# Attention over two sets of key tiles, near keys and keys of the same residue modulo four, joined by an exchange of maxima and sums

## The chip, the cores and the metric

The kernel runs on one core of a Trainium2 chip. The core has five engines that work side by side, each through its own instructions in order: TensorE (PE, matmuls and transposes; its weight loads are listed as PEld), VectorE (DVE), ScalarE (ACT), GpSimd (POOL) and SyncE (SP), which here only issues DMA transfers. PE writes into PSUM, of which the kernel's pools take eight banks of 128 partitions by 512 fp32 numbers; everything else lies in SBUF, and tensors too large for it go to DRAM and back by DMA. The metric is the device time of one execution in microseconds, as the median of several runs.

## What is computed

A block of one layer on a sequence of 1024 tokens with 1024 channels: a gated convolution branch and an attention branch, both gated and added to the input, and then a feed-forward part with a short convolution. Only the attention matters here. Each of 16 heads of 64 channels attends over three groups of keys:

```python
DILATION_GROUPS = ((128, 1), (512, 4), (2048, 16))
...
def dilated_window_attention(q, k, v, slopes, window, dilation):
    n_back = window // dilation
    ...
    scores = jnp.einsum('nbqhd,nbkhd->nbhqk', qb, kc)
    steps = (jnp.arange(ATTN_BLOCK)[:, None] + ATTN_BLOCK) - jnp.arange(2 * ATTN_BLOCK)[None, :]
    valid = (steps >= 0) & (steps <= n_back)
    ...
    dist = (steps * dilation).astype(jnp.float32)
    scores = scores - slopes[:, None, None] * dist
    scores = jnp.where(valid[None, :, None], scores, -jnp.inf)
    m = jnp.max(scores, axis=-1, keepdims=True)
    p = jnp.exp(scores - m)
    den = jnp.sum(p, axis=-1)
    o = jnp.einsum('nbhqk,nbkhd->nbqhd', p, vc) / jnp.swapaxes(den, 2, 3)[..., None]
    lse = jnp.swapaxes(m[..., 0] + jnp.log(den), 2, 3)
    return from_sub(o), from_sub(lse)
...
        mix = jax.nn.softmax(jnp.stack(lses), axis=0)
        o = jnp.einsum('gbsh,gbshd->bshd', mix, jnp.stack(outs))
```

The first group takes every key up to 128 tokens back, the second the keys of the same residue modulo 4 up to 512 back, the third those of the same residue modulo 16 as far back as there are any. Mixing the groups by the softmax of their log-sums is the same as one softmax in which a key counts once for each group that it is in; so a key's score gets the logarithm of its count added, and keys in no group are left out.

## The kernel before

All matrix products are made in fp32 halves: a factor is split into a high part of the type fp32r and the rest, the low part, and the products that matter are added up. A "split" is a copy by ACT (L86) and a subtraction by DVE (L87).

**Ahead of the attention** the projections to q, k and v are computed in tiles of 128 tokens (L150). `qkv_tail` turns each q and k tile by four PE transposes (L679) and stores high and low halves in DRAM (`dq`, `dk`); `qkv_head` stores v, high half and low half side by side, in `dv`. A first part of the gate products also lies there.

**The attention** takes the heads one after the other in eight slots each, 128 slots for 16 heads. Slot i of a head is the block of 128 queries i, and its work is:

- `score`: PE multiplies the queries with all keys of the blocks 0 to i, two matmuls (high, L776, and low half, L777, of the keys) per 512 columns; DVE (L781) adds the mask row, which holds slope, distance and logarithm of the count, and takes the row's extreme. A head has 1 + 2 + ... + 8 = 36 tiles of 128 x 128.
- `powers`: ACT takes the exponential and its row sum (L786).
- `share`, one slot later: DVE inverts the sum (L789), POOL scales the rows (L790).
- `flip`, BACK = 5 slots later: PE transposes the scaled tiles (L796) into one bank per key block and half of the queries, and ACT and DVE split the result into `ph` and `pl`.
- `weigh`, one slot after the flip: PE multiplies `ph` and `pl` with the values (L810, L811), the values' high and low halves being the 128 columns of the loaded weights; the output's upper and lower 64 rows are added in `result` (L821, L822) and stored in DRAM (`do`).

Between these PE works on **filling steps**: `side_steps` yields the remaining gate products and the output product of the convolution branch, three matmuls of 512 columns a step (L122 to L124). The table FILL says how many steps a slot takes (13.64 over the eight slots of a head), SHARE which part of them comes ahead of the flips. The halves of their weights are made beside it, one piece of 512 columns a slot: the high half by ACT (L194), the low half by POOL (L187).

The order on PE, DVE and ACT is written out by hand in the slot loop; SP's and POOL's is set by a scheduler. `head(h)` issues the seven loads of a head (queries, keys high and low for two halves of the partitions, mask), two slots into the head before it; they need the buffers of the head before that. `values(h)` loads the values. PSUM holds two double banks for scores (`psA`) and four banks (`psB`) for flips, outputs and filling steps.

**Behind the attention** `merge` multiplies the attention output with its weights and then, by DVE, with the gates (L913).

Of the kernel before, what the change touches and what calls it, by code (L numbers as in the profile page):

```python
# [21 lines left out]
P = 128  # L22
D = 1024
T = 1024
# [10 lines left out]
FILL = (1.17, 2.65, 1.40, 1.48, 1.25, 2.34, 1.64, 1.71)  # L35
# [24 lines left out]
def block_kernel(ctx: ExitStack, tc: tile.TileContext, x, xT, w_first, g1, g2, pack, mask,  # L60
# [100 lines left out]
    dv = [dr.tile([P, 8, 8, P], F32R, name=f"dv{i}") for i in range(2)]  # L161
# [20 lines left out]
    low_by = [dve]  # L182

# [6 lines left out]
    def piece_high(age=0):  # L190

        if pieces and count[2] - pieces[0][3] >= age:
            hi, lo, src, _ = pieces.popleft()
            act.activation(hi, src, AF.Copy)  # L194
            half_done.append((hi, lo, src))
# [394 lines left out]
    with tc.tile_pool(name="ph1", bufs=1, reuse_waits="tile") as p1, ExitStack() as rest:  # L590
# [65 lines left out]
        def qkv_head(ch, tt, ps):  # L656
            kind, g8 = ch % 3, ch // 3
            psv = ps.rearrange("p (h d) -> p h d", h=8)
            if kind == 2:
                vt = t4(f"v_{ch}_{tt}", F32R).rearrange("p (h s d) -> p h s d", h=8, s=2)  # L660
                split(vt[:, :, 0, :], vt[:, :, 1, :], psv)
                spill(dv[g8][:, :, tt, :], vt.rearrange("p h s d -> p h (s d)"))
# [12 lines left out]
        def qkv_tail(ch, tt, qn):  # L675
            kind, g8 = ch % 3, ch // 3
            pt = turn_ps(f"qt_{ch}_{tt}")
            for j in range(4):
                pe.transpose(pt[:, j * P : (j + 1) * P], qn[:, j * P : (j + 1) * P], ident)  # L679
# [34 lines left out]
        def head(h):  # L714
# [5 lines left out]
            m = pl.tile([P, T], F32, tag="m", name=f"m_{h}")  # L720
# [41 lines left out]
    psA = ctx.enter_context(tc.tile_pool(name="psA2", bufs=2, space=PSUM, reuse_waits="tile"))  # L762

    with tc.tile_pool(name="ph2", bufs=1, reuse_waits="tile") as p2:
        vals = {}

        def values(h):
            vals[h] = p2.tile([P, 8, P], F32R, tag="v", bufs=2, name=f"v_{h}")
            fetch(vals[h], dv[h // 8][:, h % 8, :, :])

        def score(h, tiles, i):
            q, kh, kl, m = tiles
            nk = (i + 1) * P
            s = big_ps(f"s_{h}_{i}")[:, P if i == 4 else 0 :]
            for c0, n in ((0, 384), (384, 256)) if i == 4 else [(c, min(512, nk - c)) for c in range(0, nk, 512)]:
                pe.matmul(s[:, c0 : c0 + n], q[:, i * P : (i + 1) * P], kh[:, c0 : c0 + n], start=True, stop=False)  # L776
                pe.matmul(s[:, c0 : c0 + n], q[:, i * P : (i + 1) * P], kl[:, c0 : c0 + n], start=False, stop=True)  # L777
            pt = p2.tile([P, nk], F32, tag=f"p{i}", bufs=1, name=f"p_{h}_{i}")
            st = p2.tile([P, 32], F32, tag="st", bufs=4, name=f"st_{h}_{i}")
            u0 = 896 - i * P  # L780
            dve.tensor_tensor_reduce(out=pt, in0=s[:, :nk], in1=m[:, u0 : u0 + nk], scale=-1.0, scalar=3e38,  # L781
                                     op0=ALU.add, op1=ALU.min, accum_out=st[:, 0:1])
            return pt, st

        def powers(pt, st):
# [681 lines left out]
```

## Time and profile before

| what | us |
| --- | --- |
| median of three runs | 1731.57 (1731.49 to 1732.05) |
| the profiled execution | 1732.16 |
| its span, first to last instruction | 1730.3 |
| first score to last exponential of the attention | 521.2 to 876.7 |
| ACT's last output copy of the attention | 898.4 |

The profile comes from one execution. Its page lists the busy time of each engine, the chain of work that ended last, and the costliest groups of instructions; the trace behind it can be asked for groups by line and shape, for waits, and for all instructions in order of time. A row of a timeline gives the start and the duration in us, the engine, the line, the operation, what it writes and reads, and shapes. An "idle before" behind an instruction is time in which its engine had nothing to do, with what released it; on an engine that isn't the bottleneck it costs nothing.

### The profile page before, as it was taken

What the parts mean: (1) busy time and instruction counts of PE and PEld (TensorE: products, weight loads), DVE (VectorE), ACT (ScalarE), POOL (GpSimd) and SP (SyncE); (2) the same over time, 40 slices, a digit from 0 to 9 for tenths busy, and PEclk for the clock granted to TensorE, in tenths of its full rate; (3) what the DMA queues carried; (4) which work ended last, traced back from release to release, by engine and by line L of the source; (5) the groups of instructions that cost most, each with busy time, mean ns of one, the idle gap of its engine ahead of it and who ended that gap; (6) DMA issues with size and microseconds to landing.
All of it is one profiled execution on the core that took longest, in us unless ns stands there. A gap on an engine that the chain in (4) does not pass through costs nothing.

```text
span 1730.3 us, 22656 instructions
## 1 busy us (share of the span) xinstructions
PE 1719.1 (99%) x8112; PEld 1432.8 (83%) x8112; DVE 1276.6 (74%) x1722; ACT 858.3 (50%) x1318; POOL 466.6 (27%) x351
## 2 busy tenths in 40 slices
PE   9999999999999999999999999999999999999999
PEld 7888888888888888888888888888888888888887
DVE  5999999989845666666645564887767777789863
ACT  5533345554336666776654332554445445533431
POOL 0068739999412333563410000000000000000000
PEclk9999999999999999999999999999999999999999
DMA  8232264463468656776546585622222222499851
GB/s 321 112 107 96 87 227 150 140 189 91 129 231 249 173 163 177 200 233 177 159 142 220 174 323 187 225 98 92 80 84 80 92 85 74 146 342 319 294 176 49
DMA packets 150417, 289.57 MB, mean 167 GB/s; under 512 B 12320, under 2 KB 61728, under 8 KB 150048
## 3 DMA queue, kind: packets, MB, share of 16 engines
q1 hardware_dynamic: 148576, 284.97, 50.5%
q10 hardware_dynamic: 1728, 3.15, 0.5%
q8 instruction: 64, 1.05, 0.3%
q14 instruction: 49, 0.40, 0.1%
HBM read 208.38 MB, written 79.69 MB: 166 GB/s over the span
## 4 chain that ended last, share of the span: by engine, by line
PE 96%; DMA 3%; DVE 0%; ACT 0%; issue 0%; SPq 0%; ACTq 0%
PE qkv L150 14%; PE dx L1299 7%; PE xz L130 6%; PE xz L132 6%; PE xz L131 6%; PE dy L1299 5%; PE wo L150 5%; PE pp L796 3%; PE glugv L349 3%; PE gate L122 2%; PE y L132 2%; PE y L131 2%; PE y L130 2%; PE gate L123 2%; PE gate L124 2%; PE uxz L130 2%
## 5 line engine op out<-in xcount | busy, mean ns | idle before, releaser
L630 DVE SCALAR_TENSOR_TENSOR work<-apad,pk,work 128x1024 f32<-128x1024 f32 x188 | 241.5, 1285 | 3.6
L87 DVE TENSOR_TENSOR pl<-pp,ph 128x512 fp32r<-128x512 f32 x192 | 101.1, 554 | 80.6 <-ACT ph L86 80.6
L790 POOL TENSOR_SCALAR p<-p,st 128x128 f32<-128x128 f32 (+7 forms) x128 | 96.2, 752 | 191.7 <-DVE st L789 172.3
L781 DVE CUSTOM_DVE_ANT_0 p<-s,m 128x128 f32<-128x128 f32 (+7 forms) x128 | 96.8, 756 | 55.6 <-PE s L777 42.8
L86 ACT ACTIVATE ph<-pp 128x512 fp32r<-128x512 f32 x192 | 87.3, 489 | 100.6 <-PE pp L796 99.4
L150 PE MATMUL qkv<-hi_qkv,hT 128*128 128x512 f32 x384 | 115.1, 393 | 0.0
L1202 DVE SCALAR_TENSOR_TENSOR u<-u,pk 128x1023 f32<-128x1023 f32 x88 | 112.3, 1278 | 1.0 <-ACT u L1200 0.7
L621 POOL TENSOR_TENSOR part<-prod,part 128x1024 f32<-128x1024 f32 x43 | 103.7, 2413 | 19.4 <-ACT prod L620 16.6
L786 ACT ACTIVATE p<-p,st 128x128 f32<-128x128 f32 (+7 forms) x128 | 99.2, 775 | 5.3 <-DVE st L781 2.8
L796 PE MATMUL pp<-ident,p 128*128 128x128 f32 x576 | 84.4, 273 | 0.1
L150 PEld LDWEIGHTS qkv<-hi_qkv,hT 128*128 128x128 f32 x384 | 71.4, 188 | 14.5
L796 PEld LDWEIGHTS pp<-ident,p 128*128 128x128 f32 x576 | 69.9, 140 | 15.7 <-ACT ya L248 0.3
L87 DVE TENSOR_TENSOR lo_uv<-raw_uv,hi_uv 128x1024 fp32r<-128x1024 f32 x20 | 24.5, 1226 | 78.9 <-ACT hi_uv L86 78.9
L150 PE MATMUL wo<-hi_wo,mT 128*128 128x512 f32 x256 | 80.1, 391 | 0.0
L810 PE MATMUL o<-ph,v 128*128 128x512 f32 x192 | 74.6, 392 | 0.1
L130 PE MATMUL xz<-blk_t,hi_s3g 128*128 128x512 f32 x176 | 68.6, 390 | 0.7 <-ACT xc L1176 0.7
L130 PE MATMUL xz<-h2left,hi_uv 128*128 128x512 f32 x176 | 68.7, 390 | 0.0
L132 PE MATMUL xz<-h2left,lo_uv 128*128 128x512 f32 x176 | 68.5, 389 | 0.0
L131 PE MATMUL xz<-blk_t,hi_s3g 128*128 128x512 f32 x176 | 68.5, 389 | 0.0
L132 PE MATMUL xz<-blk_t,lo_s3g 128*128 128x512 f32 x176 | 68.5, 389 | 0.0
L131 PE MATMUL xz<-h2left,hi_uv 128*128 128x512 f32 x176 | 68.5, 389 | 0.0
L150 PE MATMUL qkv<-lo_qkv,hT 128*128 128x512 f32 x192 | 68.4, 392 | 0.0
(387 smaller groups left out, 5110.0 us busy)
## 6 DMA issues: line engine op xcount, KB each, us to landing
wr<-w_down SPq DMA_DIRECT2D x45, 512.0 KB, 5.8
gr<-dff SPq DMA_DIRECT2D x62, 256.0 KB, 5.0
raw_qkv<-w_qkv SPq DMA_DIRECT2D x24, 512.0 KB, 3.9
dff<-u SPq DMA_DIRECT2D x22, 512.0 KB, 2.6
raw_uv<-w_up SPq DMA_DIRECT2D x21, 512.0 KB, 3.3
raw_ug<-w_up SPq DMA_DIRECT2D x20, 512.0 KB, 3.2
m<-mask SPq DMA_DIRECT2D x16, 512.0 KB, 7.5
q<-dq SPq DMA_DIRECT2D x32, 256.0 KB, 5.5
```

What stands on the lines that cost most here:

```text
L87: by.tensor_tensor(out=lo, in0=src, in1=hi.bitcast(F32), op=ALU.subtract)
L130: pe.matmul(o, wh[:, k, :], bh[:, k, :], start=(start and k == 0), stop=False, skip_group_check=not start)
L131: pe.matmul(o, wh[:, k, :], bl[:, k, :], start=False, stop=False, skip_group_check=not start)
L132: end = pe.matmul(o, wl[:, k, :], bh[:, k, :], start=False, stop=(k == 3), skip_group_check=not start)
L150: pe.matmul(ps, l, r[:, k % 2, :], start=(n == 1), stop=(n == 3 * KT))
L621: pool.tensor_tensor(out=a[:, CW - 1 :] if j == CW - 1 else part, in0=prods[j % 3], in1=part, op=ALU.add)
L630: dve.scalar_tensor_tensor(out=a[:, CW - 1 :] if j == CW - 1 else work, in0=a[:, j : j + T], scalar=w(c, j), in1=part if j == n else work, ...
L781: dve.tensor_tensor_reduce(out=pt, in0=s[:, :nk], in1=m[:, u0 : u0 + nk], scale=-1.0, scalar=3e38, op0=ALU.add, op1=ALU.min, accum_out=st[ ...
L786: act.activation(pt, pt, AF.Exp, bias=st[:, 0:1], scale=-1.0, accum_out=st[:, 1:2])
L796: pe.transpose(pp[:, qb * P : (qb + 1) * P], pts[qb][:, kt * P : (kt + 1) * P], ident)
L1202: dve.scalar_tensor_tensor(out=acc[:, d:], in0=src[:, : T - d], scalar=w(2 - d), in1=acc[:, d:], op0=ALU.mult, op1=ALU.add)
L1299: pe.matmul(banks[n], a[:, c], b[:, d], start=(start and i == 0 and m == 0), stop=(stop and i == nf - 1 and m == 2), skip_group_check=True)
```

## The change

The keys of a query are now taken as two sets, and each has its own row maximum and row sum.

**Near keys:** the block of the query and the one before it, n - 1 and n, so 15 tiles a head. **Keys of the same residue modulo four:** the 512 queries of one half (b = 0 or 1) and one residue r make a block of 128, with the 128 (b = 0) or 256 (b = 1) keys of that residue up to there, 4 x (1 + 2) = 12 tiles. Together 27. The mask has 512 columns, 256 per set. The first group of the reference is counted in the first set, the other two in the second.

To have the keys of one residue together, `qkv_tail` writes its transposes into PSUM so that inside a block of 128 tokens residue comes ahead of place. The queries of one residue out of four blocks are gathered on POOL (`order`), two copies a head. A slot n = 4b + r then scores near block n and residue block (b, r), both in one bank, with four matmuls and two passes of DVE and of ACT.

The rows of the two sets stand in different order over the partitions. So the maxima and sums (16 numbers per partition and set) go through DRAM: `exchange` makes two stores and two loads, and each set receives the other's numbers. MERGE = 3 slots into the next head DVE takes the common extreme (`factor_first`), ACT its exponential, and DVE the factors (`factor_last`). POOL scales the rows with them from slot 8 + BACK - 1 after the head's first on, flips begin at slot 8 + BACK, and there is one flip and one bank a slot, of 4, 3 or 2 tiles. The transposes of residue tiles write into PSUM with a step of 32, so that their columns stand in the order of the outputs. The low half `pl` meets only the high half of the values, 64 columns.

The values are fetched twice a head, in both orders. High halves of the filling steps' weights are now made by DVE in this stage. Scores and outputs share four PSUM banks (`psH`). The filling steps are spread by a table of three rates: 2.8 a slot up to slot 12, 1.53 up to the end of the scores, then 2.0.

```diff
-FILL = (1.17, 2.65, 1.40, 1.48, 1.25, 2.34, 1.64, 1.71)
+FILL = (2.8, 1.53, 2.0)
+MERGE = 3
...
             for j in range(4):
-                pe.transpose(pt[:, j * P : (j + 1) * P], qn[:, j * P : (j + 1) * P], ident)
+                pe.transpose(pt[:, j * P : (j + 1) * P].rearrange("p (r j) -> p j r", r=4), qn[:, j * P : (j + 1) * P],
+                             ident)
...
+        def order(h, b):
+            classes[h % 2, b] = t = p2.tile([P, 512], F32R, tag=f"q{b}", bufs=2 - b, name=f"q{b}_{h}")
+            q = tiles[h][0][:, 512 * b : 512 * b + 512]
+            pool.tensor_copy(t.rearrange("d (r j a) -> d r j a", a=4, r=4), q.rearrange("d (a r j) -> d r j a", a=4, r=4))
+
+        def score(h, n):
...
+            for i, k in enumerate((kh, kl)):
+                pe.matmul(s[:, c], q[:, n * P : (n + 1) * P], k[:, ks], start=(i == 0), stop=(i == 1))
+            by_class = lambda t: t.rearrange("d (i r j) -> d r i j", i=8, r=4)[:, r]
+            e = slice(256 if b else 384, 512)
+            for i, k in enumerate((kh, kl)):
+                pe.matmul(s[:, e], classes[h % 2, b][:, r * P : (r + 1) * P], by_class(k)[:, : 4 * b + 4],
+                          start=(i == 0), stop=(i == 1))
...
+        def exchange(h):
+            st = stats[h]
+            far = lambda i: dstat[i][h].rearrange("(r j) (a f) -> (j a) r f", r=4, a=4)
+            own = lambda i: st[:, i, 8:16, :].rearrange("p (r b) s -> p r (b s)", r=4)
+            sp.dma_start(dstat[0][h], st[:, 0, 0:8, :])
+            sp.dma_start(far(1), own(0))
+            sp.dma_start(own(1), far(0))
+            sp.dma_start(st[:, 1, 0:8, :], dstat[1][h])
+
+        def factor_first(h):
...
+            dve.tensor_tensor(out=w[:, 2], in0=st[:, 0, :, 0], in1=st[:, 1, :, 0], op=ALU.min)
+            dve.tensor_tensor(out=w[:, 0:2], in0=w[:, 2:3].to_broadcast([P, 2, 16]), in1=st[:, :, :, 0], op=ALU.subtract)
+            act.activation(w[:, 0:2], w[:, 0:2], AF.Exp)
...
+        def factor_last(h, w):
...
+            dve.tensor_tensor(out=st[:, :, :, 1], in0=w[:, 0:2], in1=st[:, :, :, 1], op=ALU.mult)
+            dve.tensor_tensor(out=w[:, 2], in0=st[:, 0, :, 1], in1=st[:, 1, :, 1], op=ALU.add)
+            dve.reciprocal(w[:, 2], w[:, 2])
+            dve.tensor_tensor(out=w[:, 0], in0=w[:, 0], in1=w[:, 2], op=ALU.mult)
...
+            for j, t in enumerate(srcs):
+                o = pp[:, j * P : (j + 1) * P]
+                pe.transpose(o.rearrange("p (a j) -> p j a", a=4) if j < 2 - x else o, t, ident)
...
+            for i, t in enumerate(parts):
+                m = DH if i else P
+                pe.matmul(view(o[:m]), v[:, :m], t, start=(start and i == 0), stop=(stop and i == 0),
+                          skip_group_check=True)
...
+                if n == 0 and 0 < h <= H:
+                    exchange(h - 1)
+                if n == 5 and h < H:
+                    values(h)
+                s0 = at - 7 - BACK
+                if s0 >= 0 and s0 % 8 < 7 and s0 // 8 < H:
+                    for i, k in SHARES[s0 % 8]:
+                        share(s0 // 8, i, k)
+                first = n == MERGE and 0 < h <= H
+                if first:
+                    w_now = factor_first(h - 1)
                 fill(rate * SHARE)
                 flips = []
...
+                s1 = at - 8 - BACK
+                if 0 <= s1 < 8 * H:
+                    flips.append(flip(s1 // 8, s1 % 8))
                 for w in pend:
                     done = weigh(*w) or done
                 pend = flips
-                late = None
+                if first:
+                    factor_last(h - 1, w_now)
```

The order of PE in the middle of the stage, before. One flip bank `pp` is filled by four transposes of the probabilities `p`, and the weighing adds into `o` from `ph` and `pl` (buffer numbers: head, half, key block):

```order
L796 MATMUL pp_5_0_0_5714<-ident_70,p_5_0_5520 128x128
L796 MATMUL pp_5_0_0_5714<-ident_70,p_5_1_5540 128x128
L796 MATMUL pp_5_0_0_5714<-ident_70,p_5_2_5596 128x128
L796 MATMUL pp_5_0_0_5714<-ident_70,p_5_3_5636 128x128
L810 MATMUL o_4_1_5619<-ph_4_1_6_5682,v_4_5183 128x256
L811 MATMUL o_4_1_5619<-pl_4_1_6_5683,v_4_5183 128x256
L810 MATMUL o_4_1_5619<-ph_4_1_7_5688,v_4_5183 128x128
L811 MATMUL o_4_1_5619<-pl_4_1_7_5689,v_4_5183 128x128
```

The same place in the changed kernel, with `p1` the residue tiles, `p0` the near ones, and `v1`, `v0` the values in their orders:

```order
L865 MATMUL pp_4_2_5937<-ident_70,p1_4_2_5430 128x32x4
L865 MATMUL pp_4_2_5937<-ident_70,p1_4_6_5577 128x32x4
L865 MATMUL pp_4_2_5937<-ident_70,p0_4_2_5428 128x128
L865 MATMUL pp_4_2_5937<-ident_70,p0_4_3_5458 128x128
L880 MATMUL o_4_0_5904<-ph_4_1_5900,v1_4_5539 128x4x32
L880 MATMUL o_4_0_5904<-pl_4_1_5901,v1_4_5539 64x4x32
L880 MATMUL o_4_1_5907<-ph_4_1_5900,v1_4_5539 128x4x32
L880 MATMUL o_4_1_5907<-pl_4_1_5901,v1_4_5539 64x4x32
L880 MATMUL o_4_0_5904<-ph_4_1_5900,v0_4_5538 128x256
L880 MATMUL o_4_0_5904<-pl_4_1_5901,v0_4_5538 64x256
```

Two of the four transposes now have an output in 32 steps of 4, one flip feeds both halves of the outputs, and every second matmul of the weighing has 64 output rows.

The queue of SP where the loads of a head stand, before (head 10):

```order
L156 DMA kh_10_6701<-dk1_0_80 64x1024
L156 DMA q_10_6700<-dq1_0_76 64x1024
L156 DMA kl_10_6702<-dk1_1_81 64x1024
L156 DMA q_10_6700<-dq1_1_77 64x1024
L156 DMA kh_10_6701<-dk1_0_80 64x1024
L156 DMA kl_10_6702<-dk1_1_81 64x1024
L725 DMA m_10_6703<-mask 128x1024
```

And in the changed kernel (loads of head 6, exchange of head 4, whose numbers are `st_4`, through `dst0` and `dst1` in DRAM):

```order
L157 DMA q_6_5721<-dq0_0_74 64x1024
L157 DMA kh_6_5722<-dk0_0_78 64x1024
L157 DMA kl_6_5723<-dk0_1_79 64x1024
L157 DMA q_6_5721<-dq0_1_75 64x1024
L828 DMA dst0_4_88<-st_4_5337 128x16
L829 DMA dst1_4_104<-st_4_5337 128x4x4
L157 DMA kh_6_5722<-dk0_0_78 64x1024
L157 DMA kl_6_5723<-dk0_1_79 64x1024
L830 DMA st_4_5337<-dst0_4_88 128x4x4
L831 DMA st_4_5337<-dst1_4_104 128x16
L732 DMA m_6_5724<-mask 128x512
```

The stores and the loads of the exchange now stand inside this burst, and the mask stands behind them.

DVE in the fourth slot of head 5, the changed kernel: the passes over the scores of slot 3 (`s_5_3`), the merging of head 4 (`w_4`), and between its two parts the split of a flipped tile of head 3:

```order
L815 ISA p0_5_3_5772,st_5_5642<-s_5_3_5767,m_5_5415 128x256
L815 ISA st_5_5642 128x1
L815 ISA p1_5_3_5774,st_5_5642<-s_5_3_5767,m_5_5415 128x128
L815 ISA st_5_5642 128x1
L836 TENSOR_TENSOR w_4_5776<-st_4_5337 128x16
L837 TENSOR_TENSOR w_4_5776<-w_4_5776,st_4_5337 128x32
L88 TENSOR_TENSOR pl_3_6_5788<-pp_3_6_5783,ph_3_6_5787 128x384
L843 TENSOR_TENSOR st_4_5337<-w_4_5776,st_4_5337 128x32
L844 TENSOR_TENSOR w_4_5776<-st_4_5337 128x16
L845 RECIPROCAL w_4_5776<-w_4_5776 128x16
L846 TENSOR_TENSOR w_4_5776<-w_4_5776 128x16
```

Before, a slot had one such pass, one reciprocal and its splits there, and nothing that waits for a transfer of the same head.

186 lines of the change are left out of this document (114 added, 72 removed).

## The prediction

> **What bounds the kernel now.** I read the page's head and its chain first, then the busy time by stage, then the waits of TensorE alone.
>
> ```profile
> span 1730.3 us, 22656 instructions
> ...
> PE 1719.1 (99%) x8112; PEld 1432.8 (83%) x8112; DVE 1276.6 (74%) x1722; ACT 858.3 (50%) x1318; POOL 466.6 (27%) x351
> ...
> PE 96%; DMA 3%; DVE 0%; ACT 0%; issue 0%; SPq 0%; ACTq 0%
> ```
>
> TensorE (PE) is busy for 99% of the span and makes up 96% of the chain that ended last. Next come the stage of the change (by windows: us, then PE, PEld, DVE, ACT, POOL, each busy us and count, granted clock, DMA share, GB/s) and the only wait of PE in it.
>
> ```profile
> 540.00:870.00 330.00, 328.92 (x1856) 281.70 (x1855) 209.99 (x565) 227.04 (x514) 143.05 (x162) 1.00 0.65 181
> ```
>
> ```profile
> PE s L777 <- DMA kl<-dk: 0.9, 1, 0.9
> ```
>
> In 330 us of attention PE rests for 1 us, at full clock, while VectorE (DVE) is 64% busy, ScalarE (ACT) 69%, GpSimd (POOL) 43%. So the price of the change is what it does to PE's own time, plus any new wait that reaches PE. Busy microseconds don't price a matmul, because matmuls overlap; the distance between starts does. The timeline, PE and its weight loads (PEld), start and duration in us:
>
> ```profile
> 704.47 0.49 PE L810 MATMUL o<-ph,v 128*128 128x512 f32 x1
> ...
> 704.80 0.40 PE L811 MATMUL o<-pl,v 128*128 128x512 f32 x1
> ...
> 705.04 0.40 PE L810 MATMUL o<-ph,v 128*128 128x512 f32 x1
> ...
> 709.04 0.33 PE L776 MATMUL s<-kh,q 128*128 128x384 f32 x1
> ...
> 709.21 0.34 PE L777 MATMUL s<-kl,q 128*128 128x384 f32 x1
> ...
> 709.38 0.29 PE L776 MATMUL s<-kh,q 128*128 128x256 f32 x1
> ...
> 709.51 0.28 PE L777 MATMUL s<-kl,q 128*128 128x256 f32 x1
> ...
> 709.63 0.40 PE L122 MATMUL gate<-b_again,hi_gt 128*128 128x512 f32 x1
> ...
> 709.87 0.40 PE L123 MATMUL gate<-b_again,hi_gt 128*128 128x512 f32 x1
> ...
> 720.33 0.22 PE L776 MATMUL s<-kh,q 128*128 128x128 f32 x1
> 720.34 0.19 PEld L777 LDWEIGHTS s<-kl,q 128*128 128x128 f32 x1
> 720.39 0.27 PE L777 MATMUL s<-kl,q 128*128 128x128 f32 x1
> 720.44 0.19 PEld L122 LDWEIGHTS gate<-b_again,hi_gt 128*128 128x128 f32 x1
> 720.50 0.45 PE L122 MATMUL gate<-b_again,hi_gt 128*128 128x512 f32 x1
> 720.55 0.19 PEld L123 LDWEIGHTS gate<-b_again,hi_gt 128*128 128x128 f32 x1
> ...
> 742.67 0.22 PE L776 MATMUL s<-kh,q 128*128 128x128 f32 x1
> ```
>
> From start to start: 512 columns 0.23 us, 384 0.17, 256 0.12. A matmul of 128 columns streams in 0.06 (720.33 to 720.39), but the loads behind it stand 0.10 and 0.11 apart (720.34, 720.44, 720.55), so in a row of short ones each costs the load, 0.105. The first matmul after transposes costs 0.33 instead of 0.23 (704.47 to 704.80). The last row is the first score of the next head: one head takes 742.67 - 720.33 = 22.34 us. The table FILL puts 13.64 filling steps of three 512-column matmuls beside it, 13.64 x 3 x 0.23 = 9.4 us, which leaves **12.9 us a head of attention proper**. The forms by line and one row of the chain count it:
>
> ```profile
> L776 PE MATMUL s<-kh,q x192: 218/337/442, 521.2 to 873.6; 128*128 128x512 f32 x80, 128*128 128x256 f32 x48, 128*128 128x384 f32 x48, 128*128 128x128 f32 x16
> ```
>
> ```profile
> L810 PE MATMUL o<-ph,v x192: 222/397/497, 538.3 to 897.5; 128*128 128x512 f32 x96, 128*128 128x384 f32 x32, 128*128 128x256 f32 x32, 128*128 128x128 f32 x32
> ```
>
> ```profile
> 546.03 0.87 PE pp L796 x8
> ```
>
> L777 and L811 repeat these forms with the low half. A head has 22 matmuls of 512, 10 of 384, 10 of 256 and 6 of 128: 22 x 0.23 + 10 x 0.17 + 10 x 0.12 + 6 x 0.085 (short ones stand in pairs here, 720.33 to 720.50) = 8.5 us. The 36 transposes take 36 x 0.87 / 8 = 3.9 us. Together 12.4; the missing 0.5 is the change from transposes to matmuls, eight times a head, which stays.
>
> **The change on PE.** Scores: 10 matmuls of 128 and 22 of 256, 10 x 0.105 + 22 x 0.12 = 3.7 us. The weighing: 12 of 256, 1.44 us, and 15 pairs of 128 columns, whose low half now loads only 64 columns of the values (the 64-row outputs of L880 in the changed order). A full load costs 0.105. A load of 64 columns stands nowhere in this trace: its matmul costs at least its streaming, 0.06, and at most a full load, 0.105. I take 0.06, because half of the measured load, 0.053, is below the streaming. The pairs then cost 15 x 0.165 = 2.5 us (at the upper end 3.15). Transposes: 27 x 0.109 = 2.9. So 3.7 + 1.44 + 2.5 + 2.9 + 0.5 = 11.05 us against 12.9: 1.85 a head, **29.5 us over 16 heads** (at the upper end 1.2 and 19). Notable is how little of it is columns: a quarter of the score and weigh columns goes, but the matmuls grow from 48 to 74 and become load-bound, and over half of the gain is the nine transposes, 16 us. The filling steps are the same matmuls, only spread otherwise (2.8 a slot until the first weights exist, 1.53, then 2.0): nothing.
>
> The strided outputs: 12 of the 27 transposes of a head, 192 in all, and the 128 of L679 write PSUM with a step of 32 elements.
>
> ```profile
> L679 PE MATMUL qt<-ident,qn x128: 270/272/330, 261.7 to 491.2; 128*128 128x128 f32 x128
> ```
>
> No matmul of before writes so. I bound the extra between nothing and one transpose more, 0.109, and take nothing: a transpose costs twice the 0.06 in which 128 columns stream, so its output has time to spare. [...] The strided reads and writes of keys, values and outputs keep runs of 32 elements; I cost them at nothing, with the gain or loss of a matmul hidden in the range.
>
> **The change on the other engines.** They stay beside PE as long as each has less than PE's head, 12.24 x 0.69 + 11.05 = 19.5 us. Groups by form, count, busy us and mean ns:
>
> ```profile
> L786 ACT ACTIVATION_READ_ACCUMULATOR p<-p,st 128x1 f32 x128 | 24.7, 193 | 0.0
> ...
> L786 ACT ACTIVATE p<-p,st 128x256 f32<-128x256 f32 x16 | 8.1, 504 | 0.4 <-DVE st L781 0.2
> ...
> L786 ACT ACTIVATE p<-p,st 128x128 f32<-128x128 f32 x16 | 6.3, 394 | 0.2 <-DVE st L781 0.2
> ...
> L781 DVE CUSTOM_DVE_ANT_0 p<-s,m 128x256 f32<-128x256 f32 x16 | 6.8, 422 | 6.9 <-PE s L777 6.7 <-issue 0.3
> ...
> L781 DVE CUSTOM_DVE_ANT_0 p<-s,m 128x128 f32<-128x128 f32 x16 | 4.6, 289 | 6.6 <-DMA m<-mask 2.6 <-PE s L777 2.3 <-PE pp L796 1.7
> ```
>
> ```profile
> L194 ACT ACTIVATE hi_co<-raw_co 128x512 fp32r<-128x512 f32 x16 | 10.0, 622 | 0.0
> ...
> L86 ACT ACTIVATE ph<-pp 128x512 fp32r<-128x512 f32 x96 | 53.9, 597 | 59.2 <-PE pp L796 58.0 <-ACT ya L248 0.4 <-PE o L811 0.4
> ```
>
> ACT: 16 exponentials where there were 8: 11 x 0.504 + 5 x 0.394 + 16 x 0.193 = 10.6 us a head; the splits fall by a quarter, to some 4.3 (a 512-column one is 0.597); the 0.62 us high halves of the weights go to DVE. With outputs and gates about 17 us a head of durations, as before, and durations overlap (now they fill 69% of 22.34, 15.4 us). So ACT's share rises to about 79% of 19.5. DVE: 11 x 0.422 + 5 x 0.289 and the reads, six small factor instructions, some 2.75 casts and a quarter fewer splits: about as much as now, 14.2 us, plus at most 2, so 73 to 83%. POOL has 57% rest today and gains two reorderings of the queries. None becomes the bound, but the slack of a slot (2.44 us) shrinks; I allow PE 0.3 us a head for it, 5 us.
>
> **The new wait.** DVE's minimum at L836 (L836, L838 and L880 are lines of the changed kernel) needs four transfers, two after two, and behind it on DVE stand the split of the flipped tile and the factors; behind the exponential of L838 on ACT stand the split's high half and two exponentials. PE needs that split one slot later; POOL's scaling waits for the factors, with about 3.6 us for 1.7 us of work. On SP's queue the four stand among the seven loads of the next-but-one head, whose last three or so wait behind them. Rows of that burst, and the time from issue to landing:
>
> ```profile
> 719.04 0.45 SPq L156 DMA_DIRECT2D kh<-dk  x1
> ...
> 722.78 0.53 SPq L725 DMA_DIRECT2D m<-mask  x1
> ```
>
> ```profile
> kl<-dk SPq DMA_DIRECT2D x32, 256.0 KB, 6.7
> ...
> dq<-qh SPq DMA_DIRECT2D x16, 256.0 KB, 2.6
> ```
>
> After a head's last score DVE and ACT need about 3 us. Two hops follow, each between 2.6 us (quiet) and 6.7 (in the burst): arrival 8.2 to 16.4 us after that score. DVE asks at 3 slots plus 1 us into the next head, 10.5 us after it, and PE feels it some 2.5 us later. So the hops may take 10 us. I take 9, since the burst's first half is ahead of one hop and its second half ahead of the other: no wait. Each us beyond costs 16 us. [...]
>
> **Sum.** The profiled execution took 1732.16 us, 1.9 around its span. 1732.2 - 29.5 + 5 = 1707.7; the median of before lies 0.6 below that execution, so **1707 us**.
>
> **Rivals.** *The exchange is late.* [...] One us late costs 16: 1723. Chance 0.13, half of it no longer faster. *Strided PSUM writes slow the transposes* (the other side): 320 transposes; at 0.109 more, 34.9 us, 1742, slower than before; it cancels the gain from 24.5 / 320 = 0.077 us each. [...] Chance 0.16. *The gain is smaller than its columns say:* the 64-column loads are no cheaper, or ACT's and DVE's waits take another 10 us: 1717 to 1720. For it: nothing in the trace is started faster than every 0.10 in a row. Chance 0.21. *The forecast*, 1699 to 1714: 0.50.
>
> **Numbers.** A measurement can tell 0.2%, 3.5 us. Faster: 0.50 + 0.21, and a little of the others, 0.75; the same 0.07; slower, mostly the strided writes and a late exchange, 0.18. Below 1698 would need gains nothing shows (0.05); above 1738 lie the full strided price and an exchange late by 2 us (0.13). Range 1698 to 1738; the likeliest case alone 1699 to 1714.
>
> **What would show it.** Heads 19.5 to 20 us apart; flips of four with starts 0.11 apart, strided or not (0.18 and more proves the second rival, also at L679); pairs of 128 columns 0.165 apart (0.21 is the upper end); hardly a wait of DVE at L836 on DMA, and no wait of PE on a split in the fourth slot; PE still 99% busy. Wrong I would be most simply if PE shows idle time in attention.

## The result, and the profile after

The changed kernel takes 1744.47 us (median of 4 runs, 1741.8 to 1747.96), the kernel before, beside it on the same chip, 1731.53: a ratio of 1.0076, 95% interval 1.0058 to 1.0094. It is **13 us slower**; the prediction was 1707. The profiled execution took 1747.96 us.

The head of the page and the chain that ended last, after:

```profile
span 1746.1 us, 23765 instructions
...
PE 1709.8 (98%) x8384; PEld 1427.8 (82%) x8384; DVE 1272.5 (73%) x1926; ACT 838.6 (48%) x1482; POOL 517.3 (30%) x511
...
PE 81%; DMA 11%; DVE 3%; issue 2%; ACT 1%; SPq 1%; POOL 1%; ACTq 0%; DVEq 0%; POOLq 0%
```

TensorE's share of the chain fell from 96% to 81%, and DMA has 11%. Next the busy time by windows (us, busy us and count by engine, granted clock, DMA share, GB/s) from the first score to the first product behind the attention (`yb`), before and after:

```profile
521.20:914.00 392.80, 391.72 (x2161) 334.27 (x2160) 240.19 (x622) 262.99 (x575) 151.78 (x172) 1.00 0.65 187
```

```profile
519.60:926.30 406.70, 381.86 (x2434) 330.05 (x2433) 231.76 (x822) 238.54 (x734) 200.51 (x330) 0.96 0.70 187
```

The stage grew from 392.8 to 406.7 us, 13.9 of the 15.8 us by which the two profiled executions differ. By the prediction it should have been 392.8 - 29.5 + 5 = 368.3. PE now rests for 24.8 us in it, and its clock is 0.96. What it waits for between 522 and 890 us, and what the other engines wait for there (us in total, times, longest):

```profile
PE o L880 <- ACT ph L87: 15.7, 10, 3.5
PE pp L865 <- POOL p L856: 5.5, 4, 4.7
```

```profile
DVE w L836 <- DMA st<-dst: 28.9, 13, 4.7
```

```profile
ACT w L838 <- DVE w L837: 47.9, 16, 5.2
```

```profile
POOL q L793 <- DMA q<-dq: 105.2, 14, 21.4
```

The exchange (`st<-dst`) is late in 13 of 16 heads, and PE waits for splits behind it (`ph`). One head in order of time. First PE's last score (row: start, duration) and SP's issues around it:

```profile
765.96 0.28 PE L809 MATMUL s<-kl,q 128*128 128x256 f32 x1
```

```profile
762.70 3.30 SPq L157 DMA_DIRECT2D v<-dv  x6
...
766.88 0.48 SPq L157 DMA_DIRECT2D q<-dq  x1
767.46 0.55 SPq L157 DMA_DIRECT2D kh<-dk  x1
768.10 0.55 SPq L157 DMA_DIRECT2D kl<-dk  x1
768.70 0.59 SPq L157 DMA_DIRECT2D q<-dq  x1
769.38 0.54 SPq L828 DMA_DIRECT2D dst<-st  x1
...
778.68 0.37 SPq L830 DMA_DIRECT2D st<-dst  x1
```

Then DVE, ACT and PE:

```profile
781.09 0.17 DVE L836 TENSOR_TENSOR w<-st 128x16 f32<-128x16 f32 x1 [4.18 <-DMA st<-dst]
```

```profile
781.52 0.23 ACT L838 ACTIVATE w<-w 128x32 f32<-128x32 f32 x1 [4.89 <-DVE w L837]
781.66 0.47 ACT L87 ACTIVATE ph<-pp 128x384 fp32r<-128x384 f32 x1
```

```profile
782.19 0.47 PE L880 MATMUL o<-ph,v 128*128 128x128 f32 x1 [2.61 <-ACT ph L87]
...
784.33 0.63 PE L123 MATMUL ya<-aT,hi_co 128*128 128x512 f32 x1
784.76 0.63 PE L124 MATMUL ya<-aT,hi_co 128*128 128x512 f32 x1
```

The stores go out 3.1 us after the score, behind eleven loads (six of the values, one weight piece, four of q, kh and kl); the loads of the statistics follow 9.3 us later, when the stores have landed. DVE then has waited 4.18 us, ACT behind it 4.89, and the split behind ACT's exponential lets PE run dry for 2.61. When PE goes on, 512-column matmuls start 0.43 us apart and no longer 0.23. The windows of that idle time and of the stretch behind it:

```profile
779.60:782.20 2.60, 0.01 (x1) 0.02 (x1) 0.40 (x3) 0.68 (x3) 1.22 (x1) 0.91 0.75 139
781.80:788.50 6.70, 6.20 (x23) 5.32 (x24) 4.71 (x18) 4.25 (x14) 4.80 (x10) 0.50 0.45 166
```

The granted clock is half for the 6.7 us behind a rest of 2.6. So PE loses, by an estimate from these two rows, up to half of 6.7 us, another 3.4, on top of the 2.6 that it rested.

### The profile page after: what moved, and what is told of

The parts are those of the page before. It is cut to its first block, busy times and chain, and to the rows that moved or that the text cites. A ratio compares the mean times of both kernels' runs of the same rounds, so it can differ in the third digit from the quotient of the medians.

```text
span 1746.1 us, 23765 instructions
## 1 busy us (share of the span) xinstructions
PE 1709.8 (98%) x8384; PEld 1427.8 (82%) x8384; DVE 1272.5 (73%) x1926; ACT 838.6 (48%) x1482; POOL 517.3 (30%) x511
## 4 chain that ended last, share of the span: by engine, by line
PE 81%; DMA 11%; DVE 3%; issue 2%; ACT 1%; SPq 1%; POOL 1%; ACTq 0%; DVEq 0%; POOLq 0%
PE qkv L151 14%; PE xz L131 6%; PE xz L132 6%; PE xz L133 6%; PE wo L151 5%; PE dx L1394 5%; DMA dst<-st 5%; PE dy L1394 4%; PE glugv L355 3%; PE y L132 2%; PE y L131 2%; PE y L133 2%; PE uxz L133 2%; PE uxz L132 2%; PE uxz L131 2%; PE o L880 2%
## 5 line engine op out<-in xcount | busy, mean ns | idle before, releaser
L88 DVE TENSOR_TENSOR pl<-pp,ph 128x512 fp32r<-128x512 f32 (+2 forms) x128 | 77.7, 607 | 96.6 <-ACT ph L87 96.1
L856 POOL TENSOR_SCALAR p<-p,w 128x256 f32<-128x256 f32 (+1 forms) x256 | 111.6, 458 | 54.2 <-DVE w L846 41.5
L822 ACT ACTIVATE p<-p,st 128x256 f32<-128x256 f32 (+1 forms) x256 | 118.6, 466 | 16.9 <-DVE st L815 14.9
L815 DVE CUSTOM_DVE_ANT_0 p<-s,m 128x256 f32<-128x256 f32 (+1 forms) x256 | 87.0, 377 | 33.3 <-PE s L809 30.3
L87 ACT ACTIVATE ph<-pp 128x512 fp32r<-128x512 f32 (+2 forms) x128 | 67.6, 528 | 76.0 <-PE pp L865 67.7
L880 PE MATMUL o<-ph,v 128*128 128x128 f32 (+1 forms) x336 | 84.7, 311 | 15.7 <-ACT ph L87 15.7
L880 PE MATMUL o<-pl,v 128*64 128x128 f32 (+1 forms) x336 | 77.5, 247 | 2.9 <-DVE pl L88 2.5
L880 PEld LDWEIGHTS o<-ph,v 128*128 128x128 f32 x336 | 63.1, 198 | 18.3 <-ACT ph L87 18.3
L793 POOL CAST q<-q 128x512 fp32r<-128x512 f32 x32 | 36.0, 1128 | 132.1 <-DMA q<-dq 105.2
L131 PE MATMUL xz<-h2left,hi_uv 128*128 128x512 f32 x176 | 68.7, 390 | 0.0
```

What stands on the lines that cost most here:

```text
L131: pe.matmul(o, wh[:, k, :], bh[:, k, :], start=(start and k == 0), stop=False, skip_group_check=not start)
L822: act.activation(pt, pt, AF.Exp, bias=st[:, 0, at, 0:1], scale=-1.0, accum_out=st[:, 0, at, 1:2])
L856: pool.tensor_scalar(pt, pt, f, 1.0, op0=ALU.mult, op1=ALU.mult)
L880: pe.matmul(view(o[:m]), v[:, :m], t, start=(start and i == 0), stop=(stop and i == 0), skip_group_check=True)
```

## The experiments

All have the kernel after as their base, and stand with the median, the ratio to before with its 95% interval, and the stage as above (first score to first `yb`) with PE's rest in it. The last three columns come from the one profiled execution, which can lie some us off the median (after's took 1747.96 us, e15's 1739.47).

| run | median us | ratio to before | stage us | PE busy | PE rest |
| --- | --- | --- | --- | --- | --- |
| before | 1731.5 | | 392.8 | 391.7 | 1.1 |
| after | 1744.5 | 1.0076 (1.0058 to 1.0094) | 406.7 | 381.9 | 24.8 |
| e1_no_exchange | 1719.8 | 0.9933 (0.9918 to 0.9948) | 380.0 | 370.5 | 9.5 |
| e2_one_slot_later | 1728.2 | 0.9986 (0.9976 to 0.9996) | 386.7 | 371.6 | 15.1 |
| e3_stores_on_act | 1758.8 | 1.0159 (1.0144 to 1.0174) | 421.8 | 386.0 | 35.8 |
| e4_factors_last_in_slot | 1730.1 | 0.9992 (0.9982 to 1.0003) | 390.7 | 376.2 | 14.5 |
| e5_sp_as_written | 1772.3 | 1.0238 (1.0220 to 1.0256) | 436.5 | 389.2 | 47.3 |
| e6_no_exchange_back6 | 1716.8 | 0.9913 (0.9894 to 0.9933) | 375.9 | 366.5 | 9.4 |
| e7_later_and_last_in_slot | 1731.5 | 0.9997 (0.9985 to 1.0010) | 389.8 | 374.6 | 15.2 |
| e8_all_three | 1764.7 | 1.0186 (1.0167 to 1.0204) | 424.4 | 389.4 | 35.0 |
| e10_qk_behind_stores | 1741.2 | 1.0048 (1.0032 to 1.0065) | 401.9 | 378.2 | 23.7 |
| e11_values_behind_too | 1800.7 | 1.0401 (1.0384 to 1.0418) | 459.5 | 396.4 | 63.2 |
| e12_and_a_slot_later | 1779.8 | 1.0284 (1.0266 to 1.0302) | 438.3 | 391.1 | 47.2 |
| e13_and_back6 | 1779.5 | 1.0274 (1.0255 to 1.0293) | 439.1 | 392.3 | 46.8 |
| e14_all_behind_cast_too | 1722.6 | 0.9953 (0.9936 to 0.9971) | 382.6 | 370.3 | 12.3 |
| e15_cast_behind_scaling | 1736.0 | 1.0029 (1.0018 to 1.0041) | 398.6 | 375.8 | 22.8 |
| e16_later_and_cast | 1715.8 | 0.9910 (0.9896 to 0.9925) | 376.5 | 367.7 | 8.8 |
| e17_qk_behind_cast_too | 1715.3 | 0.9910 (0.9894 to 0.9927) | 375.1 | 367.0 | 8.1 |
| e18_qk_cast_later | 1715.5 | 0.9906 (0.9890 to 0.9923) | 376.2 | 367.9 | 8.3 |
| e20_no_exchange_cast | 1710.0 | 0.9873 (0.9858 to 0.9887) | 369.2 | 364.2 | 5.0 |

### Without the exchange (e1)

```diff
-            dve.tensor_tensor(out=w[:, 2], in0=st[:, 0, :, 0], in1=st[:, 1, :, 0], op=ALU.min)
...
+            dve.tensor_tensor(out=w[:, 2], in0=st[:, 0, :, 0], in1=st[:, 0, :, 0], op=ALU.min)
...
-                if n == 0 and 0 < h <= H:
-                    exchange(h - 1)
```

> Left out: the four transfers of the exchange, so that a query's two halves are each divided by the double of their own sum and not by the joint one; the factors are worked out from the tile's own statistics with as many instructions on the vector and scalar engines as before. Theory A (the exchange's first transfers land late, the vector and scalar engines stand still until the statistics are back, the tensor engine runs dry and its clock is halved for a while): with nothing to wait for, the attention's heads stand 20 to 20.7 us apart as forecast, the clock stays at 1.00, the wait of L836 on a DMA is gone, and the time is 1705 to 1712 us. Rival B (the scalar or vector engine has too much to do in a slot, whatever the exchange does): the tensor engine still idles some 20 us in the attention, 1730 us or more. Rival C (the tensor engine's own work is dearer than forecast): no idle time and no halved clock, but the heads over 21.5 us apart, 1725 us or more.

24.7 us less than after, but 8 above theory A's range: the exchange is the larger part, and something else is left.

### More time, another place, another queue (e2, e3, e4, e7)

e2:

```diff
-MERGE = 3
-BACK = 5
+MERGE = 4
+BACK = 6
```

> MERGE 4 and BACK 6: factors, scaling and flips a slot (about 2.5 us) later, the result is unchanged. Theory A: the waits of L836 on the statistics (28.9 us over 13 of them) fall by up to 2.5 us each, to under 8 us, and the time to 1710 to 1725 us. Theory A2 (what delays the stores is the load of the values ahead of them in SP's queue, which itself waits for the end of the head before's weighing): that load moves a slot later too, so that the stores land later by as much, and the time stays within 8 us of 1744. Rival B: no change by more than 3 us.

e3:

```diff
-            sp.dma_start(dstat[0][h], st[:, 0, 0:8, :])
-            sp.dma_start(far(1), own(0))
+            act.dma_start(dstat[0][h], st[:, 0, 0:8, :])
+            act.dma_start(far(1), own(0))
```

> The two stores of the exchange are issued from the scalar engine's queue in place of SP's; the two loads stay on SP; the result is unchanged. Theory A with the queue as its cause: the stores no longer stand behind the q, k and value loads, land in about 2 us (as in the one head with nothing ahead, 2.0 us) instead of 6.2, L836 hardly waits, and the time is 1708 to 1722 us. Rival (the DMA engines are shared by all queues and full of the loads, so the store is as late from any queue): stores take 4 us or more, 1735 us or more. The scalar engine pays two issues of about 0.5 us per head: 16 us of it, beside its waits.

e4 moves both calls behind `powers`:

```diff
-                if first:
-                    w_now = factor_first(h - 1)
                 fill(rate * SHARE)
...
-                if first:
-                    factor_last(h - 1, w_now)
...
                     powers(*p)
+                if first:
+                    w_now = factor_first(h - 1)
+                    factor_last(h - 1, w_now)
```

> The same instructions; in slot 3 the factors (L836 to L838 and what follows them) are issued at the slot's end, behind the splits of the flipped tiles and the exponentials, instead of in front of them; the result is unchanged. Theory B (the place of the wait in the scalar and vector engines' order is what costs: the split and the exponentials queue behind it, and with them the flips, the weighing and the next scores): the tensor engine's waits on ph and pl in that slot go, and the time falls by 8 us or more, to 1736 or less. Theory A in its plain form (the statistics are late whatever stands around them; the scaling and the next flips wait for them): the factors come no earlier, the wait moves onto the scaling and the flips, and the time stays within 5 us of 1744.

e7 is e2 and e4 together:

> e2 and e4 together (MERGE 4, BACK 6, factors at the end of slot 4); the result is unchanged. Each alone took 14 to 16 us off. If both remove the same wait (the vector engine's for the statistics, which blocked the split behind it), the two together give no more than 5 us over the better of them: 1722 to 1729. If they remove different waits (e2 that for the statistics, e4 that of the split behind the factors), they add up in part, to 1712 to 1722.

e2 and e4 take off 16 and 14 us, e7 with both no more than each: they remove the same wait, that of the split behind the factors. Of PE's waits between 522 and 890 us, that on `ph` (15.7 us after) is nearly gone in e2 and gone in e4, and what is left stands at the scaled tiles:

```profile
PE pp L865 <- POOL p L856: 11.2, 12, 2.8
PE o L880 <- ACT ph L87: 0.8, 1, 0.8
```

```profile
PE pp L865 <- POOL p L856: 13.2, 11, 4.0
```

e3 spoke against the queue. The DMA issues (count, KB each, median us to landing), of after and of e3:

```profile
dst<-st SPq DMA_DIRECT2D x32, 8.0 KB, 6.2
st<-dst SPq DMA_DIRECT2D x32, 8.0 KB, 1.9
```

```profile
dst<-st ACTq DMA_DIRECT2D x32, 8.0 KB, 6.9
```

A store of 8 KB took 6.2 us from SP's queue and 6.9 from ACT's while the loads were under way, so the queue is not what held it. The DMA engines were full: in the head of after shown above, from the issue of the first store to that of the statistics' first load, their busy share (the last but one number) was 1.02:

```profile
769.40:778.70 9.30, 9.30 (x69) 8.38 (x68) 5.04 (x22) 5.29 (x17) 3.94 (x4) 1.00 1.02 243
```

That e3 is even slower has a reason that I only argue: SP, which no longer stops at the stores, issues more of the loads in front of the statistics' own. The trace bears this out in seven of the 16 heads; the two hops take 10.9 us in the median of the heads, against 9.0 after.

### The loads behind the stores (e5, e8, e10, e11, e12, e13)

e5 lets SP, too, follow the written order; e8 adds it to e7, with the values in slot 6:

```diff
-        with tc.manual_schedule(engines={ENG.Activation, ENG.DVE, ENG.PE}):
+        with tc.manual_schedule(engines={ENG.Activation, ENG.DVE, ENG.PE, ENG.SP}):
```

> SP's instructions stand in the order in which the code is written, as those of the scalar, vector and tensor engines do already: in each head the exchange comes first, then the q, kh, kl and mask loads of the next head (slot 2), then the values (slot 5). In the kernel after, the scheduler has four of the q and k loads and often the values ahead of the exchange's stores. The result is unchanged. Theory A (the stores are late because the DMA engines are full of the loads that went ahead of them, from whichever queue; run e3 showed that another queue doesn't help): the stores land in 2 to 3 us and not 6.2, the last statistics are back 5 to 6 us after a head's last exponential and not 9.3, L836's waits on a DMA (28.9 us) all but vanish, and the time is that of the run without exchange, 1716 to 1726 us. Rival (the time of the exchange is that of small transfers by themselves): stores stay at 5 us or more and the time at 1740 or more. Risk: SP now waits for the stores with the loads behind it; if q and k come late for the next head's scores, the time is above 1744.

> e7 with SP's instructions in written order (e5) and the values fetched in slot 6 (their buffer comes free a slot later with BACK 6); the result is unchanged. By theory A nothing is left of the exchange's wait, and the time is at or under that of the run without exchange: 1708 to 1720 us. If the loads in written order come late for the scores or the weighing, the tensor engine waits there, and it is slower than e7.

e10 only places a head's q, kh, kl and mask loads behind the stores (`held`: a new function that issues the loads behind the exchange's second store); e11 the values too:

```diff
+            with ExitStack() as behind:
+                if last:
+                    behind.enter_context(tc.issue_after(last[-1].ins))
+                return load(h)
...
-                        tiles[h + 1] = head(h + 1)
+                        tiles[h + 1] = held(head, h + 1)
...
-                if n == 5 and h < H:
-                    values(h)
+                if n == 1 and 0 < h <= H:
+                    held(values, h - 1)
```

> Only the place of some loads in SP's queue is changed, against the kernel after: the q, kh, kl and mask loads of the next head stand behind the exchange's stores, where the scheduler had four of them in front; the weights stay as early as they were (in e5 all of SP stood in written order, the stores landed in 1.6 us, but the weight tiles came late for the casts, 18.5 us of DVE's waits). The result is unchanged. Theory A: stores land in about 2 us where no value load is under way, the exchange is back 6 to 7 us after a head's last exponential, L836's waits on a DMA fall from 28.9 to under 10 us, 1722 to 1732 us. Rival (the value loads ahead are enough to hold the stores up): stores at 4 us or more, 1735 us or more.

> As e10, and the values of a head are fetched behind the exchange too, in slot 1 of the next head in place of slot 5 of their own. The result is unchanged. Theory A: the stores land in 2 us, L836 hardly waits on a DMA, and the time is that of the run without exchange or less, 1714 to 1724 us; the loads' 2.75 MB now all follow the exchange, which leaves the values 5 slots (12 us). If they come late, the tensor engine waits at the weighing on the values' load, and it is over 1730 us.

Here theory A's account of the stores held, and its forecast of the time broke. The exchange became as quick as expected: e11's first store and second store (16-byte pieces), from issue to landing,

```profile
DMA to landing us min/median/max: 1.4/1.4/3.6
```

```profile
DMA to landing us min/median/max: 2.8/3.2/4.4
```

against 2.0/6.3/9.2 and 3.3/6.0/8.8 after, and yet e11 takes 1801 us. One head of e11 shows why. The DMA engines are nearly idle when its stores go out (share 0.19):

```profile
724.00:725.80 1.80, 1.80 (x14) 1.58 (x13) 0.80 (x5) 0.55 (x3) 1.09 (x2) 1.00 0.19 9
```

DVE's last factor instruction, POOL, and PE:

```profile
735.90 0.18 DVE L854 TENSOR_TENSOR w<-w 128x16 f32<-128x16 f32 x1
```

```profile
740.07 1.05 POOL L793 CAST q<-q 128x512 fp32r<-128x512 f32 x1 [6.29 <-DMA q<-dq]
741.10 6.78 POOL L864 TENSOR_SCALAR p<-p,w 128x128 f32<-128x128 f32 x16
```

```profile
741.88 1.39 PE L873 MATMUL pp<-ident,p 128*128 128x128 f32 x4 [4.83 <-POOL p L864]
```

The factors are there at 736.1, but POOL stands at the cast of the *next* head's q (`order`), waits 6.29 us for its load, and the 16 scalings stand behind the cast. PE's waits by what ended them, in e11 and in e10:

```profile
PE pp L873 <- POOL p L864: 57.3, 14, 6.1
```

```profile
PE pp L873 <- POOL p L864: 20.0, 13, 4.7
```

So the loads moved out of the exchange's way came late for the cast (in e5, late weight tiles held DVE's casts up besides, 18.5 us in 5 waits), and the wait only changed its place. A further slot helped these kernels by 21 us and left them far behind. DVE no longer waits for the statistics in e11, so these 21 us don't speak for the rival of e12, though they lie in its range; e13 missed its own by 60 us:

> e11 with MERGE 4 and BACK 6. The result is unchanged. Theory A: with the statistics back in time in e11 already, a further slot brings little: within 5 us of e11. Rival (in e11 the wait for the statistics is still what ends last): 8 us or more under e11.

> e11 with MERGE 3 and BACK 6: the factors as early as in e11, scaling and flips a slot later behind them, as in e6 beside e1 (1716.8 against 1719.8). The result is unchanged. Theory: with the exchange in time, what is left is GpSimd's burst of scalings ahead of the flips; 2 to 6 us under e11, and the fastest of these four, 1710 to 1720. Rival: the same as e12 within 2 us.

### The cast behind the scalings (e6, e15, e17, e14, e16)

e6 asks by distance what is left without the exchange. It came out 3.0 us under e1, on the border of the rival's answer, and shows little by itself:

> Left out: the exchange, as in e1. Beside that BACK is 6 and MERGE stays 3: scaling and flips a slot later behind the factors. In e1 the tensor engine still idled 9.5 us between 522 and 890 us, mostly for tiles that GpSimd was still scaling. Theory (this rest is the distance from the factors to the flips, for GpSimd's burst of scalings): idle time under 4 us there, 1707 to 1713 us. Rival (it is the vector and scalar engines' own backlog, which the distance doesn't touch): within 3 us of e1's 1720.

e15 moves the cast alone:

```diff
-                    if n == 5 and h + 1 < H:
-                        order(h + 1, 0)
...
-                        share(s0 // 8, i, k)
+                        scaled = share(s0 // 8, i, k)
+                if n == 7 and h + 1 < H:
+                    with ExitStack() as behind:
+                        if scaled is not None:
+                            behind.enter_context(tc.issue_after(scaled.ins))
+                        order(h + 1, 0)
```

> Against the kernel after only this: GpSimd's cast of the next head's first q block stands behind twelve or so of the head's scalings (slot 7), where it stood in front of all of them (slot 5). The result is unchanged. Theory C (the cast waits for q's load, and the scalings behind it come late): in the kernel after q lands mostly before the factors are there, so little is to be had, 1738 to 1744 us. If the cast already held the scalings up there, 1732 or less.

> e10 (q, kh, kl and mask loads behind the exchange's stores) with the cast of e15. The result is unchanged. Theory C: in e10 the statistics were back early but the cast held the scalings up (20.0 us of the tensor engine's waits on scaled tiles); with the cast behind them these go below 8 us, and the time falls from 1741 to 1718 to 1728. Rival (the loads themselves, late for the scores, or full DMA engines, set the time in e10): 1736 or more.

> e11 (all of a head's loads, the values too, behind the exchange's stores) with the cast of e15. The result is unchanged. Theory C: in e11 the tensor engine waited 57.3 us for scaled tiles, 14 times, while GpSimd waited for q with the scalings behind; with the cast behind them these waits go below 15 us, and the time falls from 1801 to 1715 to 1735 us. Rival (the loads come too late for whatever needs them): 1770 or more, with the waits on q's cast now at the scores.

> e2 (MERGE 4, BACK 6; SP's order as the scheduler makes it) with the cast of e15. The result is unchanged. Theory C: in e2 what is left of the tensor engine's waits is for scaled tiles (11.2 us); q lands well before the factors there, so that moving the cast only takes its 1.1 us from in front of the scalings: 1722 to 1728. If the cast's wait counts there, under 1720.

e15 alone gives 8.4 us, more than theory C gave it and less than its other answer. e14 came out in its range, e17 3 us under its own, and e16 by its second answer, under 1720. The same move of the loads brings 3.3 us with the cast in front (after to e10, within the spread of their runs) and 20.8 with the cast behind (e15 to e17); e11 to e14, which differ by the cast alone, 78. That settles it: two queues stood in each other's way, and mending one alone shows little. What is left of the waits in e17:

```profile
DVE w L844 <- DMA st<-dst: 6.7, 3, 2.7
```

e17 and e16 are 0.9% **faster than the kernel before**, by different means against the late exchange.

### What is left (e20, e18)

e20 is e15 without the exchange; e18 is e17 with a further slot.

> Left out: the exchange, as in e1. Beside that GpSimd's cast stands behind the scalings, as in e15. If the last 8 us of e17 over the forecast are what is left of the exchange's wait, this takes 1707 to 1710 us. If they are the slots' load on the scalar and vector engines (or the tensor engine's own price), it takes 1712 to 1717, with the tensor engine idle by 5 to 9 us between 522 and 890 us for ph and pl.

> e17 with MERGE 4 and BACK 6. The result is unchanged. In e17 the vector engine still waited 6.7 us for the statistics, three times, and the tensor engine 7.4 us for ph, pl and scaled tiles. If these are one chain, the slot takes the most of it: 1708 to 1713. If it is the load of the slots, no change: 1714 to 1717. The values' buffer is then free a slot later, and their load may run into the stores again.

e20's stage, and a head's first scores, a flip of four (with two strided transposes) and its weighing:

```profile
520.10:889.30 369.20, 364.21 (x2433) 319.16 (x2432) 234.65 (x822) 239.75 (x735) 199.94 (x330) 1.00 0.75 205
```

```profile
583.12 0.22 PE L805 MATMUL s<-kh,q 128*128 128x128 f32 x1
...
584.27 0.60 PE L865 MATMUL pp<-ident,p 128*128 128x128 f32 x4
584.62 0.31 PE L880 MATMUL o<-ph,v 128*128 128x128 f32 x1
584.76 0.22 PE L880 MATMUL o<-pl,v 128*64 128x128 f32 x1
584.82 0.28 PE L880 MATMUL o<-ph,v 128*128 128x128 f32 x1
584.94 0.22 PE L880 MATMUL o<-pl,v 128*64 128x128 f32 x1
585.00 0.34 PE L880 MATMUL o<-ph,v 128*128 128x256 f32 x1
...
602.18 0.22 PE L805 MATMUL s<-kh,q 128*128 128x128 f32 x1
```

Full clock, 5.0 us of rest, a stage of 369.2 us where the prediction had 368.3. e20's 1710.0 lies within the range of the likeliest case, 1699 to 1714. The exchange still costs e17 5.2 us (1715.3 - 1710.0). e18 brought nothing more. What PE still waits for differs between the three that end at 1715 to 1716; the largest row of e16 and of e17, between 522 and 890 us:

```profile
PE s L809 <- POOL q L793: 4.4, 8, 1.1
```

```profile
PE o L888 <- DVE pl L88: 3.8, 4, 2.5
```

In e16, and in e18 with 4.2 us, it is the cast, which now stands so late that the next head's scores wait for it; in e17 it is splits. So the further slot of e18 took one wait away and brought another. That the cast's place with the later slot is what holds e16 and e18 is read from these waits alone; no run moves it back a little.

## Why the prediction was wrong

**PE's own work: right.** e20 has it without the waits: 369.2 - 5.0 = 364.2 us of work, 27.5 less than the 391.7 of before, where 29.5 was forecast. Pairs of 128 columns stand 0.20 and 0.18 apart (584.62, 584.82, 585.00), between the 0.165 that was taken and the upper end of 0.21. This head takes 602.18 - 583.12 = 19.1 us, the median of e20's heads is 19.7 (19.5 to 20 was forecast).

**Strided outputs: right at nothing.** The transposes of the projections, plain before and with a step of 32 elements after:

```profile
L685 PE MATMUL qt<-ident,qn x128: 270/272/332, 260.0 to 489.5; 128*128 128x128 f32 x128
```

272 ns as before, and the starts of transposes in a row stand 0.109 us apart in both kernels, those of the flips too (a flip of four and the step to the next matmul take 0.35, 584.27 to 584.62). The second rival's price, up to 0.109 us more for each of these transposes, is shown by no run.

**ACT's and DVE's fuller slots: right.** 5 us were allowed; e20 shows 5.0 us of rest where before had 1.1, most of it for splits. That e20's stage comes within 1 us of the forecast is luck in part: 2 us less gain on PE and 1 us less rest offset each other.

**The new wait: the step that failed**, in three places. "So the hops may take 10 us. I take 9 [...]: no wait."

1. *A middle value against a limit.* The two hops did take 9.0 us in the median of the 16 heads (from SP's first store to the last load's landing), but 5.3 to 12.0 in single heads, and DVE does come to L836 10.5 us after the last score (median of e1's heads, where no transfer holds it). With 2.8 us from the last score to the last exponential, the statistics arrive 11.9 us after the score in the median: only the supposed 2.5 us of slack behind DVE's question made that "no wait". In the head shown DVE waits 4.18 us and PE 2.61, so 1.6 us of slack were there: in the fourth slot ACT stands at L838 with the split behind it, and PE needs that split sooner than the prediction took. With 1.6 the limit is 10.5 + 1.6 = 12.1 us, which the median arrival just meets and the slower heads miss. Price of the exchange: 1744.5 - 1719.8 = 24.7 us, or with the cast behind 1736.0 - 1710.0 = 26.0. The first rival was the outcome, and its chance of 0.13 was not worked out from its bounds: of an arrival between 8.2 and 16.4 us, two fifths lie beyond the 13 that were allowed.
2. *POOL's reorderings.* They entered as busy time that POOL has to spare. Their price is their place in the queue: they wait for a load, and the scalings wait behind them. It costs 8.4 (after to e15) to 9.7 us (e1 to e20) as the scheduler placed the loads, and 78 us in e11.
3. *The price of a PE that rests.* One us late was to cost 16. But the clock was also halved behind six of the nine rests over 1 us in after's stage (counted at the end). From e20 to after, with the same matmuls, PE's rest grows by 24.8 - 5.0 = 19.8 us and its busy time by 381.9 - 364.2 = 17.7; the clock of 0.96 over 406.7 us makes up 16 of these.

Together: 1744.5 - 1707 = 37.5 us, of which 8.4 the cast (after to e15), 26.0 the exchange (e15 to e20), and 3.0 (1710.0 - 1707) the rest of the sum.

## What to carry over

The wait that was added off the bounding engine was priced by the late arrivals, head by head (DVE waited in 13 of 16 heads, up to 4.7 us), and by everything that stood in order behind each waiting instruction on its own engine; an engine with 70% rest (POOL, 30% busy in the span of after) was still the one that was late: in e11 PE waited 57.3 us for its tiles. When a remedy for a late transfer moves other transfers back, look for the in-order instruction that now waits for those, before concluding that the transfer wasn't the cause. Idle time of TensorE cost more than its length here: set against e20, each us of rest in the table above came with 0.5 to 1.4 us more of busy time.

## What the hardware showed

**Half the clock behind short rests.** Behind a rest of 1.4 us after's clock was 0.50 for 3.4 us:

```profile
710.70:712.10 1.40, 0.02 (x1) 0.00 (x0) 0.73 (x2) 0.66 (x3) 0.66 (x1) 1.00 1.04 356
713.50:716.90 3.40, 3.40 (x16) 3.10 (x16) 1.99 (x10) 2.18 (x7) 3.28 (x9) 0.50 0.48 184
```

The two stretches of half clock shown here lasted 3.4 and 6.7 us, behind rests of 1.4 and 2.6 us. Length alone didn't decide: in after's stage six rests of 1.4 to 4.7 us were each followed by half clock and three of 1.1 to 1.2 us were not, but in e17 one of 1.9 us wasn't either (the rest, and the 10 us behind it):

```profile
732.60:734.50 1.90, 0.04 (x2) 0.02 (x1) 0.40 (x3) 1.16 (x4) 0.00 (x0) 1.00 0.83 229
734.50:744.50 10.00, 9.73 (x67) 8.54 (x68) 8.55 (x25) 6.65 (x21) 8.50 (x16) 1.00 1.05 320
```

**Small stores landed later behind large loads.** In e11, with no load of q, k or v ahead, the store in pieces of 64 bytes landed in 1.4 us and that in pieces of 16 bytes, issued behind it, in 3.2 (medians); behind the loads, in after, they took 6.3 and 6.0. Whether the 1.8 us between the two come from the size of the pieces or from the place no run tells apart.
